# Where two tiles' key lists are searched, the type of a compare, and the pacing of a gathered stream, in a decoder layer on one core

## The chip, the cores and the metric

The kernel runs on one core of one Trainium2 chip. A core has TensorE (PE, with its weight loads PEld), VectorE (DVE), ScalarE (ACT), GpSimd (POOL) and SyncE (SP). SP, ACT and POOL each issue DMAs from a queue of their own, in the order of the program. The metric is the time on the device of one execution, in microseconds.

## The reference

One decoder layer for 1024 tokens of width 1024: attention of two kinds, an output projection, a second norm, and then PEER, a retrieval of experts by product keys. The change lies in PEER alone:

```python
q = (hb @ w_q).reshape(C, PEER_HEADS, 2, PEER_DK_HALF)
s = jnp.einsum('thpd,hpnd->thpn', q, sub_keys).astype(jnp.float32)
sv, si = lax.top_k(s, PEER_TOPK)
cand = sv[:, :, 0, :, None] + sv[:, :, 1, None, :]
...
fv, fpos = lax.top_k(cand, PEER_TOPK)
eidx = jnp.take_along_axis(cidx, fpos, axis=-1)
g = jax.nn.softmax(fv, axis=-1)
a = gelu(jnp.einsum('ted,td->te', u_tab[eidx], hb))
y = jnp.einsum('te,ted->td', g * a, v_tab[eidx])
```

Each token has 8 heads with two lists each. A list holds 128 key scores, of which the 16 best are kept; the 256 sums of a head's two lists give 16 experts of 16384, so 128 experts for a token.

## The kernel before

The tokens lie in 8 tiles of 128. The experts of tiles 0 to 4 (`DT = 5`) are computed densely, all 16384 of them weighted by a matrix that holds zero where an expert was not chosen. Those of tiles 5 to 7 are gathered row by row.

The stages follow one another: projections of all tokens; `block(0, 5)`, which is attention, output projection, queries and key lists of tiles 0 to 4; `block(5, 3)`, the same for tiles 5 to 7, woven in step with `route_dense`, which makes the matrices of tiles 0 to 4; and `experts()`. Up to `experts()` a scheduler sets the order on each engine by its own estimate of time. In `experts()` the order is that of the code, which was written by hand.

In `queries`, eight groups of columns each give two lists per tile: a matmul with the keys to PSUM (L775), a copy `sc` by ScalarE (L778), and `top16` (L785) for each of the two lists. `top16` is five VectorE instructions: maximum (L787), index (L788), replacement (L789), maximum (L790), index (L791).

`matrix` in `route_dense` takes four tokens at a time: VectorE makes the one-hot rows A (L881); GpSimd (L886), ScalarE (L889, L890) or VectorE (L893) make B, as the strings of `SHARE` say; TensorE multiplies (L897), ScalarE copies the product (L898), and after 32 tokens stores it to DRAM (`gd`, L900).

`routing` searches 112 sums per head with the same `top16`, and then finds which two of the 16 entries of the lists each sum came from: a compare of `ab` with `iota16` (L832), a product with the keys `sf` (L835), a sum (L836), each four times per tile over 4 heads x 16 x 16 elements.

`experts()` runs 128 passes j. In a pass, `mm_u` (L1072) makes 48 matmuls of key scores for 640 tokens, ScalarE applies Gelu (L1079), VectorE multiplies by the matrix G (L1083), `split_c` splits the result into a high part CH and a low part CL, and `mm_v` multiplies by the table v, two or three blocks of 12 matmuls per pass, four passes later. The tables come in tiles of 256 KB, two of u and two of v per pass, and are split too: the high parts uh and vh by ScalarE, the low parts ul and vl by VectorE, the first eight of either by GpSimd (L275 for all low parts).

Between these instructions `tick` puts the events of `gathered`: r (one step of `routing` of a tile), u (a product of one gathered row per token with the token, L973, on VectorE), p (coefficients), v (every fourth: the product of four gathered rows with their coefficients, L993, on TensorE) and x (the end of a tile). Tile 5's r events come first, then its u events with tile 6's r events between them, then the v events of a tile beside the u events of the next. Each event has a cost, and the stream stands at the same share of its sum as the passes do of 127:

```python
cost = [PACE[0 if t == ts[0] else 1] if kind == "u" else PACE[2] if kind == "r" else 1.0
        for kind, t, s in evs]
```

The gathers themselves (L948, 128 rows of 4 KB each) are issued on GpSimd's queue up to `NG = 7` ahead of their use, and not before a tile's routing is done; there are seven buffers.

Of the kernel before, what the change touches and what calls it, by code (L numbers as in the profile page):

```python
# [11 lines left out]
FT = mybir.dt.float32  # L12
FR = mybir.dt.float32r
I32 = mybir.dt.int32
U32 = mybir.dt.uint32
# [9 lines left out]
P = 128  # L25
NT = S // P
DT = 5
# [9 lines left out]
PACE = (1.3, 1.05, 1.5)  # L37
SHARE = ['PAPDPAPD', 'PAPDPAPD', 'PAPDPAPD', 'PDADPDAD', 'DDADPDAD']
NJ = 4
LAGS = 3  # L40
AHEAD = 2
# [7 lines left out]
def weave(*streams):  # L49
    """Trace several streams in step: each is (generator of costs, speed). None means that it waits for another."""  # L50
# [31 lines left out]
def decoder_layer(ctx: ExitStack, tc: tile.TileContext, a, out):  # L82
# [10 lines left out]
    def banks(cx, **n):  # L93
        """the banks of a phase: those of two banks each (mm), of one (pj, ov)"""
        for name, bufs in n.items():
            PS[name] = cx.enter_context(tc.tile_pool(name=name, bufs=bufs, space=PSUM, reuse_waits="tile"))
            cx.callback(PS.pop, name)
# [30 lines left out]
    # per head: nope high and low, rope [high; low]  # L128
# [3 lines left out]
    # per head and map: [high; low]  # L132
    dqd = dtile("dqd", [P, 4, 2, S])
    dkd = dtile("dkd", [P, 4, 2, S])
    vmd, vdd = (dtile(n, [NT, P, 512]) for n in ("vmd", "vdd"))
# [10 lines left out]
    iota16 = ctile([P, 16], "iota16", p=const)  # L146
# [20 lines left out]
    def rows(ap, offset, n, dst, eng=None):  # L167
        """the same row on every partition"""
        (eng or nc.gpsimd).dma_start(dst, bass.AP(tensor=ap.tensor, offset=ap.offset + offset, ap=[[0, P], [1, n]]))
        return dst  # L170
# [6 lines left out]
    def ada(g, wp):  # L177
        """two of the six vectors, 512 columns to a group of 32 columns of the array"""
# [25 lines left out]
    def mod_columns(m):  # L204
        """the first two vectors as columns"""
# [16 lines left out]
    def rstd(ss, n, name):  # L222
        """(sum of squares + n eps) ** -0.5; sqrt(n) is in the gains"""
# [22 lines left out]
    # lambda of the differential attention, on every partition  # L246
# [13 lines left out]
    def groups(ps, G, n, w, name):  # L260
        """rms factors of G groups of n columns"""
# [10 lines left out]
    def split(src, hi, lo, eng=None):  # L272
        """src = hi + lo exactly, each of 12 significant bits"""
# [3 lines left out]
    def split_scaled(src, g, hi, lo):  # L277
        """src times a factor for each partition = hi + lo"""
# [3 lines left out]
    def passes(out, ah, al, bh, bl, start, stop):  # L282
        """out += (ah + al)^T (bh + bl), without the product of the low parts' 2^-24"""
# [5 lines left out]
    def project(t0, n):  # L289
        ts = range(t0, t0 + n)  # L290
        with ExitStack() as c1:
# [31 lines left out]
            def load_up(name, K, m):  # L323
                """the weights of a second projection, split"""
# [13 lines left out]
            def rope_table(name):  # L338
                """cosines and sines with the gains in them: 64 columns for x, 64 for the cross term"""
# [37 lines left out]
            def normed(ps, n, name):  # L377
                """a latent, but for its gain"""
# [8 lines left out]
            def latent(y, n, g):  # L387
                """transposed, with its gain, split"""
# [12 lines left out]
            def heads(ps, G, n, name):  # L401
                """PSUM columns, each group scaled by its rms factor"""
# [5 lines left out]
            def rope(y, tab, G):  # L408
                """the rotated groups, split: [high, low]"""
# [12 lines left out]
            def stage(src, dst, G, dt=FR):  # L422
                """PSUM to DRAM, by way of SBUF"""
# [4 lines left out]
            def stage_split(src, dst, g):  # L428
                """four blocks in PSUM, scaled, high and low to DRAM"""
# [6 lines left out]
            def lagged(*stages):  # L436
                """stage i of a tile is traced beside stage 0 of the i-th tile after it"""
# [97 lines left out]
    def attend(t0, n, mH, mL):  # L535
        with ExitStack() as c1:
# [4 lines left out]
            # the first head's tiles (hdm, kp) lie where the projections have ended early  # L541
# [8 lines left out]
            def softmax(ps, L, l, name):  # L550
                """exponentials of one map, their sum to l"""
# [58 lines left out]
            def mixed(od, i0, e, g, f, h):  # L610
                """the heads' outputs of up to four tiles, rows scaled by f, to rows of the mixed matrix"""
# [9 lines left out]
            def unit(kind, h, i, head):  # L621
                """scores and exponentials; the transposed weights; their product with the values, in three steps"""
# [14 lines left out]
                else:  # L637
# [4 lines left out]
                    # (p1 - lambda p2 l1 / l2) / l1  # L642
# [20 lines left out]
                else:  # L663
                    # rms factors of the rows divided by l1
# [76 lines left out]
    def queries(t0, n, h2H, h2L, wp):  # L741
        N = n * P
        with ExitStack() as c1:
# [5 lines left out]
            for i in range(n):  # L749
                p = lists if t0 + i < DT else route  # L750
                R[t0 + i] = dict(sv=p.tile([P, 16, 16], FT, name="sv"), si=p.tile([P, 16, 16], U32, name="si"))
            C = N if N <= 512 else N // 2
            for cg in range(8):
# [18 lines left out]
                for i in range(n):  # L772
# [6 lines left out]
                    r = R[t0 + i]  # L779
                    for j in range(2):  # L780
# [11 lines left out]

    def routing(t, rp):
        """the 16 best pairs of each head; their experts and weights.
        Pair (a, b) of two sorted lists is behind (a + 1)(b + 1) - 1 others, in value and in order, so that
        a < 4 with any b and a >= 4 with b < 4 hold all that can be among the 16 best."""
        r = R[t]
        sv, si = r.pop("sv"), r.pop("si")
# [22 lines left out]
        ab = rp.tile([P, 2, 8, 16], FT, name="ab")  # L821
        nc.vector.scalar_tensor_tensor(ab[:, 0], pf[:, 1], -12.0, pf[:, 0], op0=OP.add, op1=OP.max)
        nc.vector.tensor_scalar(pf[:, 1], ab[:, 0], 4.0, 48.0, op0=OP.mult, op1=OP.add)
        nc.vector.scalar_tensor_tensor(pf[:, 0], ab[:, 0], 16.0, pf[:, 1], op0=OP.mult, op1=OP.min)
        nc.vector.tensor_sub(ab[:, 1], pf[:, 2], pf[:, 0])
        yield 1.2
        e = rp.tile([P, 2, 8, 16], FT, name="e")
        for q in range(2):
            for h0 in range(0, 8, 4):
                hs = slice(h0, h0 + 4)  # L830
                oh = rp.tile([P, 4, 16, 16], BF, name="oh")
                nc.vector.tensor_tensor(oh, ab[:, q, hs, :, None].to_broadcast([P, 4, 16, 16]),  # L832
# [26 lines left out]
    def route_dense(ts):  # L859
        """routing, and the weights of each token as a matrix over the two key indices, to DRAM"""  # L860
# [427 lines left out]
```

## Time and profile before

| | |
|---|---|
| median of 3 runs | 3271.18 us (3270.05 to 3275.2) |
| span of the profiled execution | 3271.8 us |
| PE busy | 3063.6 us (94%) |
| PEld busy | 2569.6 us (79%) |
| DVE busy | 2180.9 us (67%) |
| POOL busy | 1288.8 us (39%) |
| ACT busy | 1199.3 us (37%) |
| HBM read, written | 707.74 MB, 83.38 MB |

Busy shares over the whole span mix stages with different limits, so the rows below are of single stretches. An engine works in the order of its program: one that waits holds up all that stands behind it. The matmuls are pipelined and their ends are modelled, so the starts of the same instruction in two passes tell more than its busy time. The chain of waits is followed back from the end; where it stays on one engine, that engine is what the end waits for there.

### The profile page before, as it was taken

What the parts mean: (1) busy time and instruction counts of PE and PEld (TensorE: products, weight loads), DVE (VectorE), ACT (ScalarE), POOL (GpSimd) and SP (SyncE); (2) the same over time, 40 slices, a digit from 0 to 9 for tenths busy, and PEclk for the clock granted to TensorE, in tenths of its full rate; (3) what the DMA queues carried; (4) which work ended last, traced back from release to release, by engine and by line L of the source; (5) the groups of instructions that cost most, each with busy time, mean ns of one, the idle gap of its engine ahead of it and who ended that gap; (6) DMA issues with size and microseconds to landing.
All of it is one profiled execution on the core that took longest, in us unless ns stands there. A gap on an engine that the chain in (4) does not pass through costs nothing.

```text
span 3271.8 us, 49470 instructions
## 1 busy us (share of the span) xinstructions
PE 3063.6 (94%) x17865; PEld 2569.6 (79%) x17865; DVE 2180.9 (67%) x5138; ACT 1199.3 (37%) x2372; POOL 1288.8 (39%) x1197
## 2 busy tenths in 40 slices
PE   6999989988887977999999999999999999999998
PEld 3678777977776967998888888888787888887776
DVE  4767366799898987888876666655665665633334
ACT  4644383337778862223222222222222222222221
POOL 1120000004799734334444444544454545523440
PEclk9999999989898999999999999999999999999999
DMA  8653637513357655778888888888888988878884
GB/s 268 200 167 113 206 99 240 182 36 120 116 178 238 182 155 198 267 257 285 300 281 295 289 296 302 305 317 312 310 306 316 322 323 318 310 271 292 285 295 158
DMA packets 375572, 794.38 MB, mean 243 GB/s; under 512 B 31392, under 2 KB 171040, under 8 KB 368672
## 3 DMA queue, kind: packets, MB, share of 16 engines
q0 software_dynamic: 114544, 418.46, 36.5%
q1 hardware_dynamic: 153200, 311.16, 28.1%
q10 hardware_dynamic: 107584, 61.61, 6.4%
q8 instruction: 140, 2.29, 0.3%
q14 instruction: 104, 0.85, 0.1%
HBM read 707.74 MB, written 83.38 MB: 242 GB/s over the span
## 4 chain that ended last, share of the span: by engine, by line
PE 66%; DVE 9%; DMA 8%; issue 6%; ACT 4%; POOL 3%; SPq 0%; POOLq 0%; ACTq 0%; DVEq 0%
PE mm L1072 20%; PE pj L284 6%; PE pj L285 6%; PE pj L286 6%; PE y L993 5%; PE tp L284 3%; PE tp L285 3%; PE tp L286 3%; PE pg L897 3%; DMA gath<-in_peer_v,eT 2%; DMA vr<-in_peer_v 2%; POOL gath L948 2%; DVE gath L973 1%; PE ov L655 1%; POOL B L886 1%
## 5 line engine op out<-in xcount | busy, mean ns | idle before, releaser
L1072 PE MATMUL mm<-h2d,uh 128*128 128x320 f32 x4096 | 774.3, 311 | 4.8 <-ACT C L1079 4.0
L948 POOL DMA_INDIRECT gath<-in_peer_u,ei x384 | 436.1, 1136 | 730.8 <-DVE gath L973 496.8
L1072 PEld LDWEIGHTS mm<-h2d,uh 128*128 128x128 f32 x4096 | 647.3, 189 | 44.6 <-issue 25.2
L948 POOL DMA_INDIRECT gath<-in_peer_v,eT x384 | 436.5, 1137 | 336.1 <-PE y L993 191.4
L973 DVE SCALAR_TENSOR_TENSOR gath<-gath,h 128x1024 f32<-128x1024 f32 x384 | 465.4, 1223 | 91.5 <-DMA gath<-in_peer_u,ei 73.6
L1072 PE MATMUL mm<-h2d,ul 128*128 128x320 f32 x2048 | 469.1, 310 | 20.3 <-POOL ul L275 13.3
L274 ACT ACTIVATE vh<-vr 128x512 fp32r<-128x512 f32 x256 | 160.6, 629 | 691.9 <-DMA vr<-in_peer_v 358.7
L886 POOL TENSOR_SCALAR B<-iota,T 128x128 f32<-128x128 f32 x240 | 264.1, 1108 | 269.7 <-DVE T L871 198.2
L275 DVE TENSOR_TENSOR vl<-vr,vh 128x512 fp32r<-128x512 f32 x248 | 169.8, 691 | 298.4 <-ACT vh L274 232.5
L1072 PEld LDWEIGHTS mm<-h2d,ul 128*128 128x128 f32 x2048 | 343.7, 189 | 22.0 <-POOL ul L275 13.7
L1079 ACT ACTIVATE C<-mm 128x640 f32<-128x640 f32 x128 | 89.6, 700 | 570.4 <-PE mm L1072 490.1
L1083 DVE TENSOR_TENSOR C<-C,G 128x640 f32<-128x640 f32 x128 | 105.2, 822 | 254.3 <-ACT C L1079 215.5
L285 PE MATMUL pj<-vl,CH 128*128 128x512 f32 x640 | 252.3, 394 | 11.1 <-POOL vl L275 9.5
L284 PE MATMUL tp<-vh,CH 128*128 128x512 f32 x640 | 255.4, 399 | 4.8 <-DVE cT L984 2.9
L285 PE MATMUL tp<-vl,CH 128*128 128x512 f32 x640 | 252.3, 394 | 3.1 <-DVE vl L275 2.3
L284 PE MATMUL pj<-vh,CH 128*128 128x512 f32 x640 | 254.6, 398 | 0.5 <-ACT vh L274 0.3
L286 PE MATMUL tp<-vh,CL 128*128 128x512 f32 x640 | 250.5, 391 | 0.0
L286 PE MATMUL pj<-vh,CL 128*128 128x512 f32 x640 | 250.4, 391 | 0.0
L897 PE MATMUL pg<-B,A 128*128 128x128 f32 x1280 | 197.0, 301 | 51.2 <-POOL B L886 21.9
L897 PEld LDWEIGHTS pg<-B,A 128*128 128x128 f32 x1280 | 177.4, 209 | 69.3 <-POOL B L886 35.5
L274 ACT ACTIVATE uh<-ur 128x512 fp32r<-128x512 f32 x256 | 157.9, 621 | 188.9 <-DMA ur<-in_u_t 166.7
L993 PE MATMUL y<-gath,zb 128*32 128x512 f32 x1536 | 202.4, 599 | 6.1 <-DMA gath<-in_peer_v,eT 6.0
(320 smaller groups left out, 5802.3 us busy)
## 6 DMA issues: line engine op xcount, KB each, us to landing
ur<-in_u_t SPq DMA_DIRECT2D x256, 256.0 KB
vr<-in_peer_v SPq DMA_DIRECT2D x256, 256.0 KB
gd<-gs ACTq DMA_DIRECT2D x20, 2048.0 KB
G<-gd SPq DMA_DIRECT2D x31, 1280.0 KB
adaw<-in_ada_w SPq DMA_DIRECT2D x32, 512.0 KB
wraw<-in_peer_w_q SPq DMA_DIRECT2D x128, 128.0 KB
wraw<-in_w_out SPq DMA_DIRECT2D x32, 256.0 KB
wraw<-in_w_in SPq DMA_DIRECT2D x24, 256.0 KB
```

The lines of the kernel that those rows point to most:

```text
L274: nc.scalar.activation(hi, src, AF.Copy)
L275: (eng or nc.vector).tensor_sub(lo, src, hi.bitcast(FT))
L284: nc.tensor.matmul(out, ah, bh, start=start, stop=False)
L285: nc.tensor.matmul(out, ah, bl, start=False, stop=False)
L286: nc.tensor.matmul(out, al, bh, start=False, stop=stop)
L886: nc.gpsimd.tensor_scalar(B[:, m, :], iota128, T[:, 1, c + m:c + m + 1], T[:, 2, c + m:c + m + 1], op0=OP.is_equal, op1=OP.mult)
L897: nc.tensor.matmul(pg[:, o, :], A[:, o, :], B[:, o, :], start=True, stop=True)
L948: nc.gpsimd.indirect_dma_start(out=u, out_offset=None, in_=tab, in_offset=bass.IndirectOffsetOnAxis(ap=idx, axis=0))
L973: nc.vector.scalar_tensor_tensor(got[n], got[n], 1.0, q["h2"], op0=OP.mult, op1=OP.mult, accum_out=q["dots"][:, s:s + 1])
L993: nc.tensor.matmul(q["y"][RB * k:RB * k + RB, c, :], z[:, k, m % 2, RB - 1 - m:2 * RB - 1 - m], got[n + k][:, c * 512:(c + 1) * 512], star ...
L1072: nc.tensor.matmul(ps[:, o, 0:C2], s[:, k % 4, :], h2[:, mv, k, o * C2:(o + 1) * C2], start=st, stop=(k == 7 and s is l))
L1083: nc.vector.tensor_mul(c, c, gt[j // NJ][:, :, j % NJ, :])
```

## The change

The key scores of tiles 6 and 7 are no longer searched in `queries`. ScalarE's copy `sc` is stored to a tensor `scd` in DRAM, by a DMA on ScalarE's queue, two lists at a time, 16 DMAs in all. `routing` of these tiles has nine steps more in front: each loads two lists (`scl`, two buffers, on SP's queue) and searches the two that were loaded in the step before. So they have 27 r events in place of 18. The buffers of sv and si follow.

In all tiles `ab` is cast to bf16 (`abb`, one instruction more), and `iota16` is bf16, so that the compare has bf16 inputs; it wrote bf16 before.

The costs `PACE` of the first tile's u events, of the other u events and of r events become 1.45, 1.1 and 2.0. `SHARE`, the buffers and the number of gathers ahead stay. Comments leave the file, so that lines are numbered anew.

```diff
-PACE = (1.3, 1.05, 1.5)
+PACE = (1.45, 1.1, 2.0)
+LATER = (6, 7)
...
+    scd = dtile("scd", [NT, P, 16, P])
...
-    iota16 = ctile([P, 16], "iota16", p=const)
+    iota16 = ctile([P, 16], "iota16", BF, p=const)
...
-                p = lists if t0 + i < DT else route
-                R[t0 + i] = dict(sv=p.tile([P, 16, 16], FT, name="sv"), si=p.tile([P, 16, 16], U32, name="si"))
+                R[t0 + i] = {} if t0 + i in LATER else key_lists(lists if t0 + i < DT else route)
...
                     r = R[t0 + i]
+                    if t0 + i in LATER:
+                        nc.scalar.dma_start(scd[t0 + i, :, 2 * cg:2 * cg + 2, :], sc)
+                        yield 0.5
+                        continue
...
+    def key_lists(p):
+        return dict(sv=p.tile([P, 16, 16], FT, name="sv", bufs=DT if p is lists else 1),
+                    si=p.tile([P, 16, 16], U32, name="si", bufs=DT if p is lists else 1))
...
         r = R[t]
+        if t in LATER:
+            r.update(key_lists(rp))
+            got = {}
+            for c in range(0, 18, 2):
+                if c < 16:
+                    got[c] = rp.tile([P, 2, P], FT, name="scl", bufs=2)
+                    nc.sync.dma_start(got[c], scd[t, :, c:c + 2, :])
+                if c:
+                    sc = got.pop(c - 2)
+                    for j in range(2):
+                        top16(r["sv"][:, c - 2 + j, :], r["si"][:, c - 2 + j, :], sc[:, j, :], rp, P)
+                yield 3.3
...
+        abb = rp.tile([P, 2, 8, 16], BF, name="abb")
...
+        nc.vector.tensor_copy(abb, ab)
...
-                nc.vector.tensor_tensor(oh, ab[:, q, hs, :, None].to_broadcast([P, 4, 16, 16]),
+                nc.vector.tensor_tensor(oh, abb[:, q, hs, :, None].to_broadcast([P, 4, 16, 16]),
...
-        rs = {t: [("r", t, s) for s in range(18)] for t in ts}
+        rs = {t: [("r", t, s) for s in range(27 if t in LATER else 18)] for t in ts}
```

What the costs and the longer routing move shows in the order of the instructions. The first place is VectorE where the routing of tile 5 ends and the first gathered rows are used; g to ei end that routing, C, CL and ul belong to the dense passes. Before:

```order
L836 TENSOR_REDUCE e<-oh 128x64
L1083 TENSOR_TENSOR C<-C,G 128x640
L275 TENSOR_TENSOR ul<-ur,uh 128x512
L839 TENSOR_TENSOR g<-fv 128x128
L842 TENSOR_REDUCE gsum<-g 128x8
L844 RECIPROCAL grec<-gsum 128x8
L845 TENSOR_TENSOR g<-g,grec 128x128
L850 SCALAR_TENSOR_TENSOR ef<-e 128x128
L852 SCALAR_TENSOR_TENSOR ei<-e 128x128
L973 SCALAR_TENSOR_TENSOR gath,dots<-gath,h_13939 128x1024 x2
L275 TENSOR_TENSOR CL<-C,CH 128x640 x2
```

The same place on VectorE now:

```order
L860 TENSOR_REDUCE e<-oh 128x64
L278 TENSOR_TENSOR CL<-C,CH 128x640 x2
L278 TENSOR_TENSOR ul<-ur,uh 128x512
L863 TENSOR_TENSOR g<-fv 128x128
L866 TENSOR_REDUCE gsum<-g 128x8
L868 RECIPROCAL grec<-gsum 128x8
L869 TENSOR_TENSOR g<-g,grec 128x128
L874 SCALAR_TENSOR_TENSOR ef<-e 128x128
L876 SCALAR_TENSOR_TENSOR ei<-e 128x128
L1107 TENSOR_TENSOR C<-C,G 128x640
L278 TENSOR_TENSOR CL<-C,CH 128x640
L997 SCALAR_TENSOR_TENSOR gath,dots<-gath,h_13867 128x1024
```

The two CL of passes 2 and 3 have moved from behind the first gathered rows to ahead of them, and C and CL of pass 4 too.

The second place is GpSimd's queue at the start of `experts()`, low parts and gathers. Before:

```order
L275 TENSOR_TENSOR ul<-ur,uh 128x512 x8
L275 TENSOR_TENSOR vl<-vr,vh 128x512 x2
L948 DMA gath<-in_peer_u,ei 128x1024 x9
L275 TENSOR_TENSOR vl<-vr,vh 128x512 x2
L948 DMA gath<-in_peer_u,ei 128x1024 x8
```

The same place on GpSimd now:

```order
L278 TENSOR_TENSOR ul<-ur,uh 128x512 x8
L278 TENSOR_TENSOR vl<-vr,vh 128x512 x4
L972 DMA gath<-in_peer_u,ei 128x1024 x13
L278 TENSOR_TENSOR vl<-vr,vh 128x512 x2
L972 DMA gath<-in_peer_u,ei 128x1024
```

Four vl stand ahead of the first gather in place of two, and 13 gathers in place of nine ahead of the next pair.

The third place is ScalarE near the end of the queries, beside the matrix of tile 4. Before:

```order
L778 ACTIVATE sc<-tp 128x256
L890 ACTIVATE B<-B,T 128x128
L898 ACTIVATE gs<-pg 128x4x128
L889 ACTIVATE B<-iota_98,nj 128x128
L890 ACTIVATE B<-B,T 128x128
```

The same place on ScalarE now:

```order
L780 ACTIVATE sc<-tp 128x256
L277 ACTIVATE wh<-wraw 128x256
L914 ACTIVATE B<-B,T 128x128
L783 DMA scd<-sc 128x256
L922 ACTIVATE gs<-pg 128x4x128
```

The DMA of the two lists now stands between the copy of the scores and the next copy of the matrix.

## Rows read from the trace of the kernel before

**Rows 1.** Busy time by stretch: PE, PEld, DVE, ACT, POOL; clock, DMA share, GB/s.
```profile
1058.00:1130.00 72.00, 68.15 (x481) 66.65 (x480) 70.47 (x257) 64.92 (x144) 59.56 (x66) 0.98 0.62 179
1130.00:1204.00 74.00, 65.61 (x463) 61.33 (x461) 74.00 (x303) 65.24 (x140) 34.13 (x38) 1.00 0.52 147
1350.00:1500.00 150.00, 149.74 (x841) 136.26 (x841) 131.09 (x227) 39.21 (x65) 59.49 (x48) 1.00 0.81 270
1700.00:2000.00 300.00, 299.83 (x1753) 252.52 (x1752) 198.72 (x366) 70.45 (x116) 132.93 (x117) 1.00 0.84 296
2050.00:2850.00 800.00, 792.07 (x4559) 647.10 (x4558) 486.37 (x797) 181.00 (x297) 400.75 (x349) 1.00 0.88 315
2100.00:2150.00 50.00, 50.00 (x295) 40.43 (x298) 33.90 (x58) 13.55 (x22) 26.91 (x24) 1.00 0.94 341
```

**Rows 2.** Chain of waits: shares of 1117 to 1205 us; its last store.
```profile
by line: DVE B L893 31.8%; DVE A L881 25.5%; DMA gd<-gs 10.2%; DVE si L788 8.0%; DVE top L789 7.5%; DVE si L791 7.4%; DVE sv L787 6.1%; DVE sv L790 5.4%; PE pg L897 2.6%; ACT gs L898 2.4%; issue 2.1%; DVE T L871 0.5%; ACT wh L274 0.4%; DVE 
...
1204.89 8.94 DMA gd<-gs
```

**Rows 3.** Groups, 1040 to 1205 us: busy us, mean ns | idle before.
```profile
L788 DVE FIND_INDEX8 si<-sv,sc 128x8 uint32<-128x128 f32 x48 | 13.3, 281 | 0.0
L789 DVE MATCH_REPLACE8 top<-sv,sc 128x128 f32<-128x128 f32 x45 | 12.2, 272 | 0.0
L791 DVE FIND_INDEX8 si<-sv,top 128x8 uint32<-128x128 f32 x44 | 12.1, 280 | 0.0
L787 DVE MAX8 sv<-sc 128x8 f32<-128x128 f32 x48 | 11.3, 276 | 2.1 <-ACT sc L778 2.0
L790 DVE MAX8 sv<-top 128x8 f32<-128x128 f32 x44 | 11.2, 277 | 0.0
```

**Rows 4.** Timeline of ScalarE: start us, duration; first and last of twelve gs.
```profile
1095.11 1.10 ACT L898 ACTIVATE gs<-pg 128x512 f32<-128x512 f32 x1
...
1096.24 0.52 ACTq L900 DMA_DIRECT2D gd<-gs  x1
...
1119.04 1.04 ACT L898 ACTIVATE gs<-pg 128x512 f32<-128x512 f32 x1
```

**Rows 5.** Instructions of a line: ns min/median/max, first and last start.
```profile
L832 DVE TENSOR_TENSOR oh<-ab,iota x32: 1207/1218/1655, 726.4 to 1992.7; 128x1024 bf16<-128x1024 f32 x32
L835 DVE TENSOR_TENSOR oh<-oh,sf x32: 657/682/1234, 730.2 to 2018.3; 128x1024 bf16<-128x1024 bf16 x32
L819 DVE CAST pf<-pu x8: 279/294/375, 724.3 to 1850.3; 128x256 f32<-128x256 uint32 x8
```

**Rows 6.** Timeline of the expert stage's start, [idle before <-releaser].
```profile
1270.19 1.22 DVE L973 SCALAR_TENSOR_TENSOR gath<-gath,h 128x1024 f32<-128x1024 f32 x1 [8.13 <-DMA gath<-in_peer_u,ei]
...
1272.56 1.56 DVE L275 TENSOR_TENSOR CL<-C,CH 128x640 fp32r<-128x640 f32 x2
...
1274.94 3.11 POOL L275 TENSOR_TENSOR vl<-vr,vh 128x512 fp32r<-128x512 f32 x2
...
1276.42 0.79 PE L285 MATMUL pj<-vl,CH 128*128 128x512 f32 x1 [9.45 <-POOL vl L275]
```

**Rows 7.** Chain of waits, three passes on TensorE: start us, us.
```profile
1368.35 7.04 PE mm L1072 x48
...
1383.57 7.04 PE mm L1072 x48
...
1396.07 7.04 PE mm L1072 x48
```

**Rows 8.** The page's group of the gathered products; all Gelu of a line.
```profile
L993 PE MATMUL y<-gath,zb 128*32 128x512 f32 x1536 | 202.4, 599 | 6.1 <-DMA gath<-in_peer_v,eT 6.0
...
L1079 ACT ACTIVATE C<-mm x128: 682/704/708, 1225.5 to 3222.1; 128x640 f32<-128x640 f32 x128
```

**Rows 9.** DMA issues: count, KB each.
```profile
ur<-in_u_t SPq DMA_DIRECT2D x256, 256.0 KB
...
G<-gd SPq DMA_DIRECT2D x31, 1280.0 KB
```

## The prediction

> **What bounds the kernel now.** Words first: a *pass* is one of the 128 rounds j of the expert loop, a *list* is one search for the 16 best of 128 key scores, and a *turn* is four u steps and one r step of the gathered stream. I read the busy times by stage, then the chain of waits, then single lines. The expert stage takes two thirds of the span, and TensorE sets its pace. Two passes of the stage in a quiet stretch begin 15.22 and 12.50 us after the one before [rows 7]: 48 score matmuls take 7.04 us, the rest are three or two blocks of the value product. So a pass costs 13.86 us on average; the products of the gathered rows come on top, 202.4 us for 96 groups of four rows, 2.11 each [rows 8]. The 127 intervals between the first and the last Gelu need 4 x 7.04 + 123 x 13.86 + 202 = 1935 us, and they take 3222.1 - 1225.5 = 1997 [rows 8]. About 61 us is therefore all the idle time of TensorE in that stage. The largest single piece, 9.45 us, stands at the start [rows 6].
>
> Before it, between 1058 and 1204 us, the queries of tiles 5 to 7 run beside the dense routing matrices. VectorE is busy in 70.5 of the first 72 us and in all of the last 74 [rows 1], and the chain of waits runs through VectorE alone there, ending with the last store of the matrix (8.94 us), for which the expert stage waits [rows 2]. That is where the change takes work away. But the neighbours are close behind: TensorE 68.2 and 65.6 us, ScalarE 64.9 and 65.2 [rows 1].
>
> **The change part by part.** *Lists out of the matrix stage.* A list is five VectorE instructions: 11.3/48 + 13.3/48 + 12.2/45 + 11.2/44 + 12.1/44 = 1.31 us [rows 3]. 32 of the 48 lists leave, 42 us, and of them somewhat over half, some 22, in the last 74 us. VectorE would then need 52 of 74, so it no longer ends last; ScalarE does. It gains 16 DMA issues; the only issue in this stage took 0.52 us [rows 4], so they cost up to 8.3 us in all, half in either part. ScalarE's floor becomes 65.2 + 4.2 = 69.4 of 74 and TensorE's 68.2 of 72, so the two parts can give back at most 4.6 + 3.8, about 8 us. Where ScalarE already ran without a gap it made 11 copies of the matrix in 1119.04 - 1095.11 = 23.9 us, 2.18 each [rows 4]; the last 74 us hold the 32 of tile 4, 2.31 each. At 2.18 they would take 69.8, and the issues take most of that back. Bounds: -8 (all of it) and +4 (no gain in pace, half the issues exposed). I take **-3**, near the ScalarE rows. Everything behind the last matrix moves with it.
>
> *The choice among 16 in bf16.* One instruction of 1024 elements took 1.218 us with f32 inputs and the product after it, bf16 throughout, 0.682 [rows 5]. The new compare lies between these, four per tile, plus one cast of 256 elements, 0.29 us by the nearest row [rows 5]. That is between -1.9 and +0.3 us per tile, and only tile 5's stands ahead of something that is waited for, the first gather. I take the upper row, the same shape with one value held over 16 columns: **+0.3**. [...]
>
> *The other shares, at the start.* An event of cost c moves the stream by 127 c / N passes, N being the sum of all costs: 921.2 before; after, 72 r steps x 2.0 + 128 x 1.45 + 256 x 1.1 + 384 + 21 = 1016.2. Tile 5's routing (18 r steps) thus ends at pass 4.5 instead of 3.7. Before, the first u product stood ahead of both CL of passes 2 and 3, waited 8.13 us for its row, and the eighth and ninth gather held GpSimd's next vl behind that product: CL at 1272.56, vl at 1274.94, and TensorE idle until 1276.42 [rows 6]. In the new order CL stands ahead of the first u product, and all four vl ahead of the gathers. The 9.45 us go, but for about 1 us in which the raw v rows land. With fewer routing steps ahead of them two splits come some 2 us sooner. What is late next: the second ul of pass 5 stands behind the first u product, which still waits about 8 us for its row, with two blocks (5.6 us) and half a score product (3.5 us) as cover on TensorE; I put 3 us on that. Behind that, 13 gathers now stand ahead of vl of the next half, and they need six u products; with a pass of cover I put nothing. Bounds -11 and 0; **-8**.
>
> *Lists in the expert stage.* They come back as 16 lists in eight r steps of tile 6 and as many of tile 7. The second eight lie where VectorE is two thirds busy (198.7 of 300 us [rows 1]): nothing. The first eight lie where it is busy 131 of 150 us, 87% [rows 1]. There a turn was 6.7 units = 0.924 pass = 12.8 us, 11.2 of them busy; now it is 7.8 units = 0.975 pass = 13.5 us, with two lists in place of one, 11.2 + 1.3 + 0.3 for the longer turn = 12.8, 95%. The average still fits, but two lists in a row hold ul and vl back by 2.6 us. Bounds 0 and +8; **+3**. The 16 loads (128 KB) go on SP's queue. Each waits for the lists two r steps earlier, with the next ur, vr and G loads behind it; a turn of 13.5 us lies between, so nothing is added; without that cover it would be a late ur.
>
> *Later shares.* Since the routing takes more of the stream, the rest runs closer. Four v and four u rows were 8.2 units = 1.13 pass, and become 8.4 units = 1.05 pass: 7.62 gathers of 512 KB to a pass, not 7.08, from about pass 71 to 109. A pass also loads four 256 KB tiles and a quarter of 1280 KB [rows 9], 1.38 MB. So 5.37 MB in 13.86 + 0.95 x 2.11 = 15.9 us, 338 GB/s, where 2050 to 2850 us shows 315 at a DMA share of 0.88 [rows 1]. 341 GB/s at 0.94 occurs, for 50 us [rows 1]. TensorE's own waits for gathered rows are short so far, 6.0 us in all [rows 8]. Bounds 0 and +21 (the third rival); I take **+6**, low because 341 is seen and because tile 7's longer routing thins out passes 37 to 71.
>
> Sum: -3 + 0.3 - 8 + 3 + 6 = -1.7, on the profiled execution's span of 3271.8, itself 0.6 above the median of the runs (3271.18). **Forecast: 3269 us.**
>
> **Rivals.** *First, the relief passes and nothing is given back*: -8 in the matrix stage, -11 at the start, 0 for lists and shares, 3252; with half of the later terms, 3257. For it: VectorE alone is on the chain for 84 us [rows 2]. Against: ScalarE at 65 of 74. *Second, VectorE becomes the bound in passes 5 to 14*: if a list costs 1.6 us with its value loads and the turn exceeds 13.5 us, TensorE waits for ul and vl; eight turns x 1 us = +8 in place of +3, 3274. *Third, slower: the DMA queues fill*. If from pass 71 on they still move only 315 GB/s, a pass takes 5.37 MB / 315 = 17.05 us; over 37 passes that is 43 us above the 15.9 of TensorE, less the 0.3 a pass that was idle anyway and the 6 counted, and less what earlier, thinner passes save (some 5): +21, 3290. It decides from the point where the bytes per microsecond stop rising with the share; for it speaks the 0.88, against it the 341. *Fourth, bf16 does nothing or halves the compares*: 3269 or 3267.
>
> **How the numbers follow.** About 0.2% (6.5 us) is what a measurement of this kernel can tell from no change. Forecast and second rival, 3264.6 to 3277.7: 0.42. First rival and cases near it: 0.36, as the start alone may give 8 and the other terms may be nothing. Third rival and milder forms of it: 0.22. The range of 8 in 10 goes from the first rival's end to just short of the third's, 3251 to 3288; the likeliest case's own is 3265 to 3278.
>
> **What would show it.** In the trace after: VectorE clearly below full between 1058 us and the last store, with ScalarE at 95% or more and that store 2 to 4 us sooner; no 9 us hole on TensorE ahead of the first vl; VectorE over 93% in the ten passes behind it, with waits for ul or vl; compares at 1.2 us; 325 GB/s or more in the passes with seven and a half gathers. Wrong if the last store comes 10 us or more sooner (ScalarE was not the next bound), if the hole only moves to the next half pass, or if the later passes stretch beyond 16.5 us.

## The result and the profile after

| | before | after |
|---|---|---|
| median of the runs | 3270.61 us (3268.51 to 3275.2, 4 runs) | 3303.82 us (3298.47 to 3310.07, 4 runs) |
| span of the profiled execution | 3271.8 us | 3308.3 us |
| first to last copy of the routing matrix | 437.5 us | 446.5 us |
| first to last Gelu of the expert stage | 1996.7 us | 2019.5 us |

The change makes the kernel slower, by a factor of 1.0096 with an interval of 1.008 to 1.0111. The forecast was 3269 us with a range up to 3288. Of the 36.5 us between the two profiled spans, 9.0 lie in the matrix stage and 22.8 in the expert stage. Another 6.6 lie ahead of the first copy, where no edit reaches. The other kernels below reach that copy at 766.9 to 775.4 us, so those 6.6 are scatter of single executions. Between the last copy and the first Gelu lie 0.6 us more, and after the last Gelu 2.5 us are saved. The copies before (those after follow below) and the Gelu after (those before are in [rows 8]), with first and last start:

```profile
L898 ACT ACTIVATE gs<-pg x160: 1009/1080/1182, 766.3 to 1203.8; 128x512 f32<-128x512 f32 x160
...
L1103 ACT ACTIVATE C<-mm x128: 682/704/710, 1241.6 to 3261.1; 128x640 f32<-128x640 f32 x128
```

The matrix stage, from the trace of the kernel after: all copies of the matrix, the 16 stores of key scores with their issue time on ScalarE's queue (ns min/median/max), and the busy times in the stretches of tiles 3 and 4.

```profile
L922 ACT ACTIVATE gs<-pg x160: 1007/1086/1182, 772.9 to 1219.4; 128x512 f32<-128x512 f32 x160
L783 ACTq DMA_DIRECT2D scd<-sc x16: 326/326/8507, 1062.9 to 1216.8; - x16
1059.50:1149.00 89.50, 70.37 (x468) 68.23 (x468) 55.75 (x157) 66.81 (x150) 58.00 (x64) 0.90 0.60 176
1149.00:1220.50 71.50, 65.92 (x474) 64.94 (x472) 58.90 (x193) 63.63 (x138) 38.14 (x39) 0.98 0.61 176
```

VectorE, full before [rows 1], is busy in 55.8 of 89.5 us. But nobody else is full in its place: ScalarE is busy in 66.8. The profile puts 9.77 us of its idle time there down to no other engine ("issue"), and the longest issue on its own queue took 8.51 us in that time. The timelines of ScalarE and TensorE there:

```profile
1059.56 0.53 ACTq L924 DMA_DIRECT2D gd<-gs  x1
...
1062.91 8.51 ACTq L783 DMA_DIRECT2D scd<-sc  x1
1071.47 1.03 ACT L922 ACTIVATE gs<-pg 128x512 f32<-128x512 f32 x1 [9.77 <-issue]
```
```profile
1060.98 1.60 PE L921 MATMUL pg<-B,A 128*128 128x128 f32 x12
1072.59 3.75 PE L921 MATMUL pg<-B,A 128*128 128x128 f32 x16 [10.01 <-issue]
```

A store of 128 KB that stands on ScalarE's queue 3.4 us behind a 2048 KB store of the matrix keeps ScalarE from its next instruction for 8.5 us. The next copy of the matrix waits, its PSUM bank with it, and so do TensorE (10.01 us), VectorE (8.83) and GpSimd (11.20). Three more issues took 3.27, 5.19 and 5.46 us, each within 3 us behind such a store; the other twelve took 0.33 to 0.78.

The expert stage. For each pass I took the time between the last score products of two passes and subtracted 7.06 us for the scores, 2.775 for each value block and 1.95 for each group of gathered rows, as they cost in undisturbed passes. What is left is TensorE's lost time, in us by passes (an undisturbed pass comes out within 0.4 of zero, mostly just below):

| passes | 1–5 | 6–15 | 16–71 | 72–80 | 81–108 | 109–127 |
|---|---|---|---|---|---|---|
| before | 24.5 | 0.9 | 9.4 | 9.5 | 8.8 | 8.7 |
| after | 13.7 | 14.1 | 6.0 | 13.0 | 24.1 | 13.0 |

*The start* gained 10.8 us. The hole of 9.45 us [rows 6] is gone; the first gathered row holds VectorE for 3.80 us and TensorE for 1.46:

```profile
1290.91 1.23 DVE L997 SCALAR_TENSOR_TENSOR gath<-gath,h 128x1024 f32<-128x1024 f32 x1 [3.80 <-DMA gath<-in_peer_u,ei]
...
1292.81 0.56 PE L1096 MATMUL mm<-h2d,ul 128*128 128x320 f32 x2 [1.46 <-DVE ul L278]
```

*Passes 6 to 15* lost 13.2 us, in every second pass from 9 to 15 (3.9, 3.7, 4.8, 1.7). In the timeline of VectorE the two lists of an r step stand in one piece from 1406.82 to 1409.98, 1.58 us each, ahead of ul and the u products. The ul after that stands behind one more ul, three u products, C and CL, and TensorE waits 2.38 us for it:

```profile
1406.82 0.29 DVE L793 MAX8 sv<-scl 128x8 f32<-128x128 f32 x1
...
1409.78 0.28 DVE L797 FIND_INDEX8 si<-sv,top 128x8 uint32<-128x128 f32 x1
1409.98 0.67 DVE L278 TENSOR_TENSOR ul<-ur,uh 128x512 fp32r<-128x512 f32 x1
...
1416.37 0.69 DVE L278 TENSOR_TENSOR ul<-ur,uh 128x512 fp32r<-128x512 f32 x1
...
1419.32 0.29 DVE L793 MAX8 sv<-scl 128x8 f32<-128x128 f32 x1
```
```profile
1417.11 0.56 PE L1096 MATMUL mm<-h2d,ul 128*128 128x320 f32 x2 [2.38 <-DVE ul L278]
```

The load of the next two lists does not hold up SyncE's queue here. It is issued while the present lists are still being searched, and the load of ur behind it goes out as soon as VectorE is done with the ul of 1409.98:

```profile
1407.31 0.43 SPq L814 DMA_DIRECT2D scl<-scd  x1
1410.68 0.33 SPq L1061 DMA_DIRECT2D ur<-in_u_t  x1
```

*From pass 72 on* 50.1 us are lost in place of 27.0. The largest single hole is at pass 76, where the stream goes from tile 6's coefficients to tile 7: VectorE stands for 12.47 us at a u product whose row h has not landed, and TensorE waits behind it. SyncE issued h at 2363.33, right behind a G of 1280 KB and an output of 512 KB. The timelines of VectorE, TensorE and SyncE:

```profile
2375.59 1.23 DVE L997 SCALAR_TENSOR_TENSOR gath<-gath,h 128x1024 f32<-128x1024 f32 x1 [12.47 <-DMA h<-h2d]
...
2377.48 0.48 PE L1006 MATMUL tp<-ident,co 128*128 128x128 f32 x1 [9.43 <-DVE yd L1129]
```
```profile
2362.22 0.34 SPq L1029 DMA_DIRECT2D out<-gath  x1
2362.95 0.33 SPq L1088 DMA_DIRECT2D G<-gd  x1
2363.33 0.80 SPq L995 DMA_DIRECT2D h<-h2d  x1
```

Passes 72 to 77, around this change, lose 13.0 us in place of 6.6. The rest is spread: by the groups of the two pages TensorE's waits for gathered rows are 10.7 us in place of 6.0 [rows 8], and VectorE's for u rows 105.5 in place of 73.6 (first line before, the others after). The stretch from 2600 to 2900 us moves 323 GB/s at a DMA share of 0.90 where the kernel before moves 312 at 0.88, by the busy times in the second fence, before and after. The change of tiles and TensorE's own waits make up some 6 and 5 of the 23.1 us; for the others no single wait stands out.

```profile
L973 DVE SCALAR_TENSOR_TENSOR gath<-gath,h 128x1024 f32<-128x1024 f32 x384 | 465.4, 1223 | 91.5 <-DMA gath<-in_peer_u,ei 73.6
...
L997 DVE SCALAR_TENSOR_TENSOR gath<-gath,h 128x1024 f32<-128x1024 f32 x384 | 464.6, 1224 | 134.2 <-DMA gath<-in_peer_u,ei 105.5
...
L1017 PE MATMUL y<-gath,zb 128*32 128x512 f32 x1536 | 208.2, 605 | 10.7 <-DMA gath<-in_peer_v,eT 10.7
```
```profile
2600.00:2900.00 300.00, 297.93 (x1729) 244.88 (x1729) 177.82 (x290) 68.15 (x112) 138.68 (x124) 1.00 0.88 312
2600.00:2900.00 300.00, 295.16 (x1685) 236.56 (x1684) 181.20 (x298) 65.59 (x108) 160.58 (x139) 0.99 0.90 323
```

*The choice among 16* needs no experiment; the two lines in the trace after, compare and new cast:

```profile
L856 DVE TENSOR_TENSOR oh<-abb,iota x32: 1199/1219/2314, 735.1 to 2241.7; 128x1024 bf16<-128x1024 bf16 x32
...
L849 DVE CAST abb<-ab x8: 278/292/375, 734.6 to 2100.7; 128x256 bf16<-128x256 f32 x8
```

The compare takes 1219 ns, as with f32 inputs [rows 5], and the cast adds 0.29 us per tile. So +0.3 holds, and the fourth rival's halved compare is out. Why bf16 inputs bring the compare nothing is not shown.

### The profile page after: what moved, and what is told of

It is laid out like the page before. It is cut to its first block, busy times and chain, and to the rows that moved or that the text cites. A ratio compares the mean times of both kernels' runs of the same rounds, so it can differ in the third digit from the quotient of the medians.

```text
span 3308.3 us, 49516 instructions
## 1 busy us (share of the span) xinstructions
PE 3067.9 (93%) x17865; PEld 2569.6 (78%) x17865; DVE 2196.8 (66%) x5146; ACT 1197.9 (36%) x2371; POOL 1292.1 (39%) x1197
## 3 DMA queue, kind: packets, MB, share of 16 engines
q1 hardware_dynamic: 155504, 313.26, 28.3%
## 4 chain that ended last, share of the span: by engine, by line
PE 48%; DMA 7%; DVE 5%; issue 3%; POOL 1%; ACT 1%; ACTq 0%; SPq 0%; POOLq 0%; DVEq 0%
PE mm L1096 20%; PE y L1017 5%; PE pj L287 4%; PE pj L288 4%; PE pj L289 4%; PE tp L287 3%; PE tp L288 3%; PE tp L289 3%; DMA gath<-in_peer_v,eT 3%; DMA vr<-in_peer_v 3%; DVE gath L997 2%; POOL gath L972 1%; DMA gath<-in_peer_u,ei 1%; PE pg L921 1%; DMA h<-h2d 1%
## 5 line engine op out<-in xcount | busy, mean ns | idle before, releaser
L997 DVE SCALAR_TENSOR_TENSOR gath<-gath,h 128x1024 f32<-128x1024 f32 x384 | 464.6, 1224 | 134.2 <-DMA gath<-in_peer_u,ei 105.5
L1096 PE MATMUL mm<-h2d,ul 128*128 128x320 f32 x2048 | 470.2, 311 | 20.1 <-POOL ul L278 12.8
L1096 PEld LDWEIGHTS mm<-h2d,ul 128*128 128x128 f32 x2048 | 343.9, 189 | 22.9 <-POOL ul L278 13.3
L1017 PE MATMUL y<-gath,zb 128*32 128x512 f32 x1536 | 208.2, 605 | 10.7 <-DMA gath<-in_peer_v,eT 10.7
```

Of the source, the lines that this page charges most:

```text
L997: nc.vector.scalar_tensor_tensor(got[n], got[n], 1.0, q["h2"], op0=OP.mult, op1=OP.mult, accum_out=q["dots"][:, s:s + 1])
L1017: nc.tensor.matmul(q["y"][RB * k:RB * k + RB, c, :], z[:, k, m % 2, RB - 1 - m:2 * RB - 1 - m], got[n + k][:, c * 512:(c + 1) * 512], star ...
L1096: nc.tensor.matmul(ps[:, o, 0:C2], s[:, k % 4, :], h2[:, mv, k, o * C2:(o + 1) * C2], start=st, stop=(k == 7 and s is l))
```

## The experiments

Three theories were left after the traces. *T1*: issues behind the matrix's stores hold ScalarE and turn a gain of the matrix stage into a loss. *T2*: pairs of lists on a VectorE that is nearly full stall passes 6 to 15. *T3*: the late losses come from the spacing of the gathered rows, since more routing steps push the rows closer together. Rivals: the order of the instructions (T1), the shares (T2), the lists themselves or the shares alone (T3). Single runs of one kernel scatter by some 10 us to either side, so times are given as ratios to the kernel before measured beside them (median 3277.87 us for the first four, 3274.19 for the next three, 3270.68 for the last four), and what happens inside is read from the traces, one execution of each kernel.

**One edit: the queue of the stores.**

```diff
-                        nc.scalar.dma_start(scd[t0 + i, :, 2 * cg:2 * cg + 2, :], sc)
+                        nc.sync.dma_start(scd[t0 + i, :, 2 * cg:2 * cg + 2, :], sc)
```

> The changed kernel with one edit: the 16 stores of key scores (scd<-sc) are issued by SyncE, not by ScalarE. First theory: four of those issues, each behind a 2048 KB store of the routing matrix on ScalarE's queue, held ScalarE for 8.5, 3.3, 5.2 and 5.5 us, 22 us in all, and that is where the matrix stage lost its 15.6 us. Then the last copy of the matrix, at 1219.4 us in the changed kernel, comes at 1204 to 1209, no hole of 10 us stands after 1062, and the time falls by 10 to 16, to 3288 to 3294. Rival: the stage is longer because the instructions were put in another order, with ScalarE as the bound: the last copy stays past 1214 and the time above 3299.

Measured: 3278.66 us, ratio 1.0004 (0.9985 to 1.0023). First to last copy 419.9 us, and the last copy begins at 1187.9. The copies, the stores and the stretches of tiles 3 and 4 in this kernel's trace:

```profile
L922 ACT ACTIVATE gs<-pg x160: 1007/1080/1167, 768.0 to 1187.9; 128x512 f32<-128x512 f32 x160
L783 SPq DMA_DIRECT2D scd<-sc x16: 319/326/1005, 1056.8 to 1187.2; - x16
...
1054.80:1124.30 69.50, 66.30 (x474) 64.27 (x475) 56.03 (x160) 65.83 (x148) 58.40 (x64) 1.00 0.76 221
1124.30:1189.00 64.70, 62.91 (x466) 62.37 (x465) 59.93 (x185) 62.71 (x138) 35.05 (x40) 1.00 0.67 196
```

The same 16 stores beside the same 2048 KB stores take at most 1.0 us to issue, and ScalarE is busy 95 and 97% of the time. T1 holds and was too small: the issues cost 446.5 - 419.9 = 26.6 us, because the relief underneath is 437.5 - 419.9 = 17.6, not the few us that the first reading of the trace suggested. The order as the cause is out. The expert stage is about as long as in the changed kernel (2018.0 us between the Gelus, 21.3 above the kernel before), so what it lost has other causes. By the passes of the table it loses 14.2, 16.5, 8.8, 13.2, 18.6 and 12.4.

**The stores without the move of the lists**, in the kernel before (nobody reads what is stored):

```diff
+                    if t0 + i >= 6:
+                        nc.scalar.dma_start(scd[t0 + i, :, 2 * cg:2 * cg + 2, :], sc)
```

> The kernel before with only the 16 stores of the key scores of tiles 6 and 7 added on ScalarE's queue; the lists stay where they were and nobody reads what is stored. First theory (an issue behind a 2048 KB store holds ScalarE for 3 to 8 us): the matrix stage grows by 8 to 16 us and the time is 3279 to 3287. Rival (issues cost 0.5 us each, as the prediction had it): at most 4 us more, 3275 or less.

Measured: 3283.59 us, ratio 1.0017 (1.0005 to 1.0028); first to last copy 444.8 us, +7.3. Four issues took 3.83, 4.03, 2.71 and 2.56 us. The copies, and one of the issues on ScalarE's timeline:

```profile
L901 ACT ACTIVATE gs<-pg x160: 1007/1078/1167, 770.0 to 1214.8; 128x512 f32<-128x512 f32 x160
```
```profile
1101.07 3.83 ACTq L782 DMA_DIRECT2D scd<-sc  x1
...
1104.94 0.49 ACT L771 ACTIVATE qh<-pj 128x384 f32<-128x384 f32 x1 [3.22 <-issue]
```

The stores alone make the stage longer, but by 7.3 us, a little under the expected 8 to 16. VectorE, the bound here, stays busy through the four held issues (13.15 of 13.2 us), so part of the hold costs nothing. The time is 5.7 us above the kernel before, between the two expectations.

**The shares, undone and alone.** In the changed kernel:

```diff
-PACE = (1.45, 1.1, 2.0)
+PACE = (1.3, 1.05, 1.5)
```

> The changed kernel with the old shares of the gathered stream (1.3, 1.05, 1.5). If the new shares crowd the rows of the later tiles and cost what passes 76 to 110 lost (about 20 us of stalls), those stalls mostly go, and the hole of 9 us ahead of the first vl is back: 3288 to 3296. Rival: the late stalls come from the lists, which thin out the middle of the stream whatever the shares are: then they stay, the early hole comes on top, and the time is 3306 to 3314.

Measured: 3331.93 us, ratio 1.0162 (1.0139 to 1.0185); the profiled execution (span 3309.4) is the fastest of five, so what the others lose besides was not traced. Both expectations are missed on the high side. Lost by the same passes: 27.6, 7.6, 17.8, 7.6, 22.9, 11.0. The start is back at its old loss, and 81 to 108 still lose 22.9. So the new shares help this kernel, and most of what it loses late does not come from them (41.5 us from pass 72 on with the old shares, 50.1 with the new, 27.0 in the kernel before). And in the kernel before, the opposite edit:

> The kernel before with nothing but the new shares (1.45, 1.1, 2.0). The matrix stage should be as before (last copy of the matrix near 1204). If the shares do at the start what the prediction said, the 9 us hole ahead of the first vl goes, 8 to 10 us. If they also cost the late stalls, 15 to 20 us come back after pass 71: 3275 to 3282. Rival (the late stalls are not from the shares): 3258 to 3266.

Measured: 3269.6 us, ratio 0.9976 (0.9957 to 0.9995). Lost: 14.8, 0.1, 9.4, 9.2, 13.2, 10.9. The start gives 9.7, passes 6 to 15 do not stall, and from 72 on 6.3 are lost. In microseconds the time lies between the two expectations; beside the kernel before (3277.87 here) it is 8.3 lower, as far as the rival had put it. The shares alone are a gain.

**Which tile's lists.** Both with the stores on SyncE; the list tiles come from the routes' pool, so that all fits:

```diff
-LATER = (6, 7)
+LATER = (7,)
```

> The changed kernel with the stores on SyncE and only tile 7's lists in the expert stage; tile 6's are searched beside the routing matrix again (its list tiles come from the pool of the routes, so that all fits). Theory: two lists to each r step, on a VectorE that was 87% busy, are what stalled passes 9 to 15 by 13 to 16 us. Then passes 6 to 15 lose under 3 us, the last copy of the matrix comes at 1190 to 1198, and the time is 10 to 20 below the kernel before of the same chip. Rival (the stalls of passes 9 to 15 come from the new shares or the order of the loads): they stay above 8 us, and the time is within 5 of the kernel before.

Measured: 3271.87 us, ratio 0.9997 (0.9979 to 1.0015). First to last copy 422.2 us. Lost: 13.3, 5.1, 8.6, 12.4, 12.3, 19.8; pass 7 alone has 6.4, and passes 9 to 15 lose nothing, where the changed kernel loses 14.0 there and 12.7 with its stores on SyncE. The same 90 us in the changed kernel and in this one, whose passes come 22 to 37 us earlier there, TensorE's busy time first:

```profile
1350.00:1440.00 90.00, 82.86 (x448) 71.88 (x447) 75.56 (x188) 20.55 (x34) 29.95 (x24) 1.00 0.67 222
```
```profile
1350.00:1440.00 90.00, 90.00 (x514) 82.69 (x513) 78.38 (x143) 23.33 (x38) 31.99 (x28) 1.00 0.77 259
```

T2 holds: without tile 6's lists TensorE has no gap there. (Their loads leave with them; that it is the searches rests on the timelines above.) VectorE is *less* busy in the stalling kernel (75.6 of 90) than in the other (78.4): its share does not show a pair of lists that comes at the wrong moment. The time, though, missed the expected 10 to 20 us, since passes 72 to 127 still lose 44.5. The complement:

```diff
-LATER = (6, 7)
+LATER = (6,)
```

> The complement: stores on SyncE, only tile 6's lists in the expert stage, tile 7's beside the routing matrix. Theory: passes 6 to 15 lose 12 us or more as in the changed kernel, but tile 7's routing has 18 steps again, the rows of the later tiles are spread wider (1.07 passes for eight of them, not 1.05), and passes 81 to 108 lose 10 to 16 in place of 19 to 24: time 0 to 8 below the kernel before. Rival (late stalls have nothing to do with how closely the rows follow): passes 81 to 108 lose as much as in the changed kernel.

Measured: 3286.08 us, ratio 1.005 (1.0031 to 1.0069). Lost: 13.2, 8.6, 13.8, 16.7, 13.9, 17.9. Passes 9 to 15 stall again, by less than expected (8.4 us, why less stays open). The late passes lose 48.5 together, no better than with tile 7's lists: the expected relief in 81 to 108 came (13.9) and was lost in the passes around it. The time, expected 0 to 8 below the kernel before, is 11.9 above it.

**The spacing of the rows.** The kernel with only tile 7's lists, and an r step of tiles 6 and 7 counted 1.2:

```diff
-        cost = [PACE[0 if t == ts[0] else 1] if kind == "u" else PACE[2] if kind == "r" else 1.0
+        cost = [PACE[0 if t == ts[0] else 1] if kind == "u" else (PACE[2] if t == ts[0] else 1.2) if kind == "r" else 1.0
```

> As the one with only tile 7's lists in the expert stage, and an r step of tiles 6 and 7 counts 1.2 in place of 2.0 (tile 5's stays at 2.0): eight rows of the later tiles take 1.11 passes, about as before the change (1.13). If late stalls follow from the rows' spacing, passes 81 to 108 lose 8 to 12 us, as in the kernel before (8.8), and the time is 3 to 10 below the run beside it with 2.0. Rival: no difference there, and a turn of four u steps and an r step is shorter (7.0 units), so passes 6 to 15 lose 3 to 6 more.

Measured: 3265.34 us, ratio 0.9979 (0.9961 to 0.9996). Lost: 10.6, 9.4, 8.9, 11.4, 8.6, 8.3. The waits for rows by its page, and the late stretch:

```profile
L997 DVE SCALAR_TENSOR_TENSOR gath<-gath,h 128x1024 f32<-128x1024 f32 x384 | 466.1, 1226 | 93.1 <-DMA gath<-in_peer_u,ei 78.8
...
L1017 PE MATMUL y<-gath,zb 128*32 128x512 f32 x1536 | 198.8, 599 | 5.7 <-DMA gath<-in_peer_v,eT 5.5
```
```profile
2600.00:2900.00 300.00, 298.66 (x1732) 245.63 (x1730) 179.52 (x294) 70.38 (x116) 138.88 (x124) 1.00 0.89 317
```

Passes 72 to 127 lose 28.3 us, 16 less than beside it with 2.0, at fewer bytes per microsecond (325 there); a second execution, below, loses 36.7, 8 less. The rival's other half came as well: passes 6 to 15 lose 4.3 us more than with 2.0. Over all kernels, by the passes that eight rows (four u, four v) take, which follows from the sum of all costs:

| kernel | passes for eight rows | lost in 72–127 |
|---|---|---|
| before; stores alone | 1.13 | 27.0; 24.1 |
| tile 7's lists, light routing; again | 1.11 | 28.3; 36.7 |
| shares with light routing alone (below) | 1.12 | 36.3 |
| old shares; row h earlier (below) | 1.10 | 41.5; 29.8 |
| shares alone | 1.09 | 33.3 |
| tile 7's lists; tile 6's lists | 1.07 | 44.5; 48.5 |
| after; again; stores on SyncE | 1.05 | 50.1; 49.2; 44.2 |

T3 holds as a tendency: from 1.09 passes up the loss is 24 to 37 in all kernels but one, closer it is 44 to 50. The old shares, which lie above their place, show that spacing is not all; a change of tiles at pass 108 cost 9.6 there. Nor do VectorE's waits for u rows decide: with shares alone its page has 127.2 us of them, more than the changed kernel's 105.5, and 33.3 are lost. How close rows turn into lost time, beyond the change of tiles, is not shown. The version with light routing and the changed kernel were each measured once more:

> The kernel with tile 7's lists moved, stores on SyncE and light routing steps once more, to stand beside the others of this call: 6 to 12 under the kernel before, passes 81 to 108 losing under 12.

Measured: 3266.63 us, ratio 0.9981 (0.9968 to 0.9993). Passes 81 to 108 lose 12.2; this and the 4.1 us below the kernel before just miss what was expected. This version is faster than both kernels, by 0.2% against the kernel before in either measurement, with intervals that just exclude no change. Its hole at the start has moved: passes 6 and 7 lose 7.2 and 11.8 us in its two executions, and 8.4 in the one below that moves no list, where the kernel before loses 1.1.

> The changed kernel once more, beside the kernel before on the same chip: 28 to 38 slower, four issues of the key-score stores again of 3 to 9 us each on ScalarE's queue, passes 6 to 15 losing 12 to 16, passes 81 to 108 losing 18 to 26, the change of tiles at pass 76 again over 8.

Measured: 3306.73 us, ratio 1.0094 (1.0076 to 1.0112). Lost: 13.0, 12.8, 4.2, 14.5, 21.4, 13.3, with 9.4 at pass 76; first to last copy 446.9 us, and four of the stores' issues are held again, for 2.34 to 7.01 us. So the holes of the changed kernel belong to it and not to one execution:

```profile
L783 ACTq DMA_DIRECT2D scd<-sc x16: 326/327/7009, 1070.5 to 1219.8; - x16
```

**Is a moved list worth anything?** The kernel before with the shares of that version, no list moved, the compare in f32:

> The kernel before with shares only: 1.45, 1.1, 2.0 for tile 5, and 1.2 for an r step of tiles 6 and 7; no list is moved, the compare stays as it was. If moving tile 7's lists is worth what the matrix stage showed (about 10 us less up to the last copy), this is 5 to 10 slower than the run of this call with tile 7's lists moved, so within 3 of the kernel before or up to 5 faster. Rival (the moved lists cost in the expert stage what they save before it): equal to that run, 8 to 12 faster than the kernel before.

Measured: 3273.77 us, ratio 0.9997 (0.9982 to 1.0012). First to last copy 435.9 us against 422.0, and the time is 7.1 us above the version beside it, as expected. So moving one tile's lists looks like a net gain, but a small one: the two intervals overlap.

**The row h of the next tile earlier**, on top of that version:

```diff
-AHEAD = 2
+AHEAD = 0
...
             elif kind == "p" and s == 0:
+                if t != ts[-1]:
+                    load_h(t + 1)
```

> As the run with tile 7's lists moved and light routing steps, and the row h of the next tile is loaded at the first p step of the present one, with no u product between the p steps. Theory: at the change from one tile to the next VectorE stands at the first u product until h has landed (12 us in the changed kernel at pass 76), and ul, vl and the coefficients wait behind it. Then the stalls at passes 31 to 36 and 72 to 77, 15 us together, fall below 6, and the time is 5 to 10 under the run beside it. Rival (those stalls come from the gathers around the change): they stay, within 3 of the run beside it.

Measured: 3269.64 us, ratio 0.999 (0.9978 to 1.0002). The holes go as expected: passes 31 to 36 and 72 to 77 lose 4.8 us in place of 17.1 in the first run of that version. The time does not follow: 81 to 108 lose 16.0, not 8.6 to 12.2, with rows at 1.10 in place of 1.11, and the time, expected 5 to 10 below that version, is 3.0 above it. What is saved at the change of tiles is mostly lost further on; why, beyond the slightly closer rows, stays open.

## Why the prediction was wrong

**What bounds the matrix stage: right.** VectorE was the bound, and without its lists the stage is 17.6 us shorter once nothing else is in the way. **The size was wrong, and the step that failed is the price of the issues.** "[T]he only issue in this stage took 0.52 us [rows 4], so they cost up to 8.3 us in all": this priced sixteen issues by one of a matrix store, and those go out 14.6 us or more apart in the kernel before. Some of them were to go close behind stores whose landing, 8.94 us, stood in [rows 2]. Measured: 22.4 us in four held issues, and 26.6 us of the stage. The bounds, -8 to +4, held neither: the stage ended at +9.0, the sum of -17.6 and +26.6. The -8 failed as well. It took ScalarE's 65.2 us in a window of 74 as the floor for tile 4, while that tile's copies need 70.2 and ScalarE was busy for 62.4 of them; and some 6 us of the gain lie ahead of any list that moved: tile 1's copies take 100.0 us in the changed kernel and 108.1 before, and so in every kernel of this study, 100 to 104 with moved lists, 107 to 108 without. The order of the instructions differs there; this was not separated.

**The start: right**, -8 forecast, -10.8 measured, for the reason given: shares alone give 9.7. The first u product waited 3.80 us for its row, not the 8 forecast.

**Lists in the expert stage: right in mechanism, mis-sized.** +3 forecast (0 to +8), 13.2 measured, in passes 9 to 15, which lose nothing when tile 6's lists stay out; that tile 7's would add nothing there was right. The second rival named its condition, "if a list costs 1.6 us with its value loads", and a list takes 1.58. But it is not the average that decides, as the step assumed (11.2 + 1.3 + 0.3 of 13.5): a pair of lists is 3.16 us in one piece, and the pairs above stand 12.5 us apart. The forecast of "over 93%" for VectorE was wrong: 84%, and TensorE still waited.

**Later shares: the third rival's size, in part by another way.** +6 forecast, bounds to +21, 23.1 measured. The queues did not stop at 315 GB/s as the rival had it; they moved 323. But the kernels whose rows follow most closely lose most, and the wider spacing of the light routing steps takes 8 to 16 us back; through which waits is only shown in part. The reason for taking the low value, "341 is seen", looked at bytes and not at how late a row comes at that rate. The tile change at pass 76 was not priced at all.

**The sum.** The adverse terms were seen as rivals with chances of their own, but three of them came together, and the range was made as if at most one would. From the profiled spans the stages give 9.0 - 10.8 + 13.2 - 3.4 + 23.1 = 31.1 us, where the prediction's sum was -1.7; the other 5 us are the 6.6 ahead and small differences at the ends.

## What to carry to other kernels

Before a DMA issue is put on a compute engine's queue, look at what stands ahead of it on that queue: up to 4 us behind a 2048 KB store it held the engine here for 2.3 to 8.5 us, not the 0.33 to 0.78 us of the changed kernel's other twelve, and SyncE's queue took such stores in 1.2 us or less. A step moved onto an engine that is 87% busy is to be priced by its longest piece and by who waits behind that piece, not by the average that still fits. When work is added to a stream that is spread over a fixed number of passes, everything behind it comes closer together, and that can be a cost of its own.

## What the runs showed of the hardware

- **Four issues behind a 2048 KB store on ScalarE's queue took 3.27 to 8.51 us, the same stores on SyncE's queue at most 1.0.** Four more were held in the kernel with the stores alone, for 2.56 to 4.03 us. Seven of the eight held issues, in the changed kernel and in the one with the stores alone, end 6.05 to 6.57 us after the issue of the 2048 KB store ahead (1108.06 + 3.27 - 1105.25 = 6.08, for one); three of them, in the changed kernel, 3.1 to 3.8 us before that store landed. The eighth ends 11.9 us after its store, which took 14.6 to land. The changed kernel's second execution has 6.14, 6.27, 6.57 and, for the first held issue, 8.02. From SyncE's queue the same stores issue in 0.3 to 1.0 us beside the same traffic, and in at most 1.2 us where only tile 7's are stored. So only the queue with the 2048 KB stores held its issuer; by what is not shown.
- **Behind a hole of 10 us TensorE was slower for some microseconds.** In the 11 us ahead of the hole at 1062 the granted clock is 1.00. In the first 4.5 us after the 10 us without a matmul it is 0.50, in the next 5 us 0.93, and from 1082 to 1090 1.00 again: 16 matmuls behind the hole take 3.75 us, 0.23 each, 12 of the same kind ahead of it 1.60, 0.13 each. Two stretches behind the hole, the eighth column is the clock:

```profile
1072.50:1077.00 4.50, 4.41 (x21) 4.44 (x22) 2.02 (x6) 4.33 (x10) 1.74 (x2) 0.50 0.34 106
1077.00:1082.00 5.00, 4.28 (x30) 4.09 (x30) 4.39 (x14) 4.80 (x11) 4.51 (x5) 0.93 0.11 35
```
